# Routing of two expert layers: places with experts on partitions, slots ahead of the gates, router products in two column halves

## The chip, the cores and the metric

The kernel runs on one core of a Trainium2 chip: TensorE (PE; PEld is its weight load), VectorE (DVE), ScalarE (ACT), GpSimd (POOL), SyncE (SP, which here only issues DMAs), and 16 DMA engines. The metric is the device time of one execution in microseconds (us). Lower is better.

## The reference, cut to what matters

Two transformer blocks in a row on 512 tokens of width 1024 in fp32. Each block ends in a routed expert layer:

```python
# block 1: 32 experts in 4 groups; a token takes the best group and its two best experts
gates = jnp.sum(jax.nn.one_hot(e_idx, N_EXPERTS) * e_weight[..., None], axis=1)
...
hid = silu(hf @ w_g[e]) * (hf @ w_u[e]) * gates[:, e]
out = out + hid @ w_d[e]
# block 2: 64 experts in 8 groups, six experts a token, and one expert that all tokens share
shared = (jax.nn.silu(xf @ w_sh_gate) * (xf @ w_sh_up)) @ w_sh_down
return (shared + routed).reshape(B, S, D)
```

Every expert has three matrices of 1 MB (1024 x 256, 1024 x 256, 256 x 1024), so the first layer reads 96 MB of weights and the second 192 MB. Everything in front of the expert layers (attention of two kinds and a gated recurrence in block 1, two attentions and modulation in block 2) is untouched by the change.

## The kernel before

The 512 tokens are four tiles of 128 rows (`NT`). An expert layer is one `Moe` object: `phase_b` builds the one of 32 experts, `phase_d` with `rest_d` that of 64.

Router. As each tile of the residual is done, `head(t)` normalises it and writes it to DRAM (`hD`); the tile is transposed on PE (`xt`) and `logits(t)` multiplies it by the router's weights: eight fp32 matmuls a tile with the 128 x 128 token block as the weights in the array and 36 (block 1) or 64 (block 2) columns moving (bank `lg`). VectorE then picks groups and experts and leaves a one-hot matrix, `A` in block 1 and `Ab` in block 2, tokens on partitions, and the gates `G`.

Places. `positions` counts the tokens of each expert (`cnt`), and `rank` sorts the experts by their counts into a permutation matrix `P`; `perm` (its list) lets SP address the weights of the expert of rank r. Static loads (the first `STATIC` experts) need no `perm`. `positions` then makes each token's place within its expert: ten bf16 matmuls (`pos`), `posm`, four transposes (`posT`), a copy, a matmul by `P` that sorts the rows by rank (`posR`) and a cast. `ranked` transposes the gates (`GT`), sorts them by rank (`Gr`) and writes them to DRAM (`gD`).

Units. The experts are worked in units of 128 slots, `UNITS1` and `UNITS2`; a unit is shared by one to three experts of known ranks (64 + 64, 96 + 32, ...). `pick(u)` makes a matrix `sel` that names the rank of each slot, `prep(u)` calls `slots`: `bc` broadcasts the place row of each slot's expert (one fp32r matmul), VectorE compares it with the slot's number (`st`) and sums the token number out of it (`jk` is the scratch output, `ii` the number), and two indirect DMAs on POOL's queue gather the 128 token rows (`xg` from `hD`) and their gates (`gg` from `gD`). `turn` transposes the rows on PE (`xT`); `hidden` multiplies by the gate and up matrices (`g`, `u`), takes silu on ScalarE and the product with the gate on VectorE (`hid`), and transposes that (`hT`); `down` makes `y`; `scatter` adds it back with `st` as the matrix (`sc`).

Order. The code is written once in an order and a planner, run when the program is built, fixes each engine's queue from it: an instruction that is ready and stands earlier in the code goes first, `high_priority` moves a part up, `issue_after` puts one behind another, and `manual_schedule` keeps the units' PE and VectorE queues as written. Tiles live in rooms by tag: all tiles of a tag share its buffers. Of pool `moe` matter here: `hid` (one buffer; the tiles `hid` and `jk`), `xT` (one buffer; `xT`, and in block 2 the shared expert's `hTx`), `st` (four), `yh`, `yl` and `sel` (two each). `Carve` lends the rooms of `st`, `yh` and `yl` to the router's small tiles until the units need them. PSUM has two rings of four banks, `bank` and `pbank`; `lg`, `g`, `u`, `y` and the shared expert's `hT` come from `pbank`.

In block 1, `rest` calls `positions`, `ranked` and `run`. `run` picks and preps units 0 and 1, then lets `fetch(3, after=self.gathered.ins, free=NF)` release the rest of unit 2's loads: a one-element memset on POOL in each weight buffer stands behind the last gather of unit 1, and the load behind the memset. In block 2, `rest_d` calls `positions` and `ranked`, then traces the shared expert (`hidden` and `down` over four tiles), and only then `run`. The shared expert needs the normalised tiles (`hTs`) and nothing of the routing.

## Time and profile before

| | |
|---|---|
| time, median of 3 runs | 1671.65 us (1668.68 to 1672.71) |
| the profiled execution's own time | 1676.92 us |
| its span, first to last instruction | 1675.2 us |
| granted TensorE clock, mean share of full | 0.971 |
| busy: PE, PEld, DVE, ACT, POOL | 93%, 63%, 58%, 32%, 21% |
| DMA | 420.78 MB, mean 251 GB/s |
| first expert layer: router to the last unit | about 350 to 610 us |
| second expert layer: router to the end | about 1055 to 1675 us |

A share of busy time is a mean over the whole span. The stages differ, so the stages are read by their own windows and timelines. A matmul counts as busy from its start to its modelled end, so a PE that is busy throughout may still be waiting for its clock, which has two levels here, 1.0 (2.4 GHz) and 0.5 (1.2 GHz).

### The profile page before, as it was taken

The page shows a single profiled execution, that of the slowest core. Times are in us where ns is not written, and L with a number is a line of the kernel's source. Part 1 is how long each engine was busy: PE and PEld are TensorE (multiplying, and loading weights), DVE is VectorE, ACT ScalarE, POOL GpSimd, SP SyncE. Part 2 cuts the span into 40 slices and gives each one's busy share as a digit, 9 for nine tenths or more (in the row PEclk, how much of TensorE's full clock was granted, in tenths as well). Part 3 has the DMA queues.
Part 4 walks back from the last instruction along what each step waited for, and adds up shares of the span by engine and source line. Part 5 has one row for each costly group of instructions (what it writes and reads, how often), then busy time and mean ns, then how long its engine had stood idle before and what let it go on. Part 6 is the DMA issues. An engine that isn't in the chain of part 4 may idle for free.

```text
span 1675.2 us, 28638 instructions
## 1 busy us (share of the span) xinstructions
PE 1550.9 (93%) x10917; PEld 1060.7 (63%) x10917; DVE 970.1 (58%) x2219; ACT 542.3 (32%) x1090; POOL 347.4 (21%) x287
## 2 busy tenths in 40 slices
PE   5899999978998877899999998999999999999996
PEld 5665557765565546675667777865666666666663
DVE  3598536853564348547455534555665665656656
ACT  4534676331211125555553322301211211112112
POOL 2323551012111103330104441131111101111000
PEclk9999999987999998999999999899999999999998
DMA  5443336468999953233006837748899999999961
GB/s 187 147 162 114 107 82 233 132 214 321 418 416 417 419 239 105 72 104 90 26 5 203 255 104 276 285 168 366 366 411 386 396 412 415 418 414 422 419 259 64
DMA packets 104207, 420.78 MB, mean 251 GB/s; under 512 B 23444, under 2 KB 30074, under 8 KB 66692
## 3 DMA queue, kind: packets, MB, share of 16 engines
q1 hardware_dynamic: 82880, 389.25, 60.5%
q0 software_dynamic: 9968, 19.04, 3.1%
q10 hardware_dynamic: 11220, 10.63, 2.0%
q8 instruction: 87, 1.43, 0.3%
q14 instruction: 52, 0.43, 0.1%
HBM read 419.99 MB, written 9.21 MB: 256 GB/s over the span
## 4 chain that ended last, share of the span: by engine, by line
PE 46%; DVE 5%; DMA 4%; POOL 1%; ACT 1%; issue 1%; SPq 0%; DVEq 0%; ACTq 0%; POOLq 0%
PE g L973 8%; PE u L973 8%; PE sc L1051 7%; PE y L997 7%; PE qk L1671 2%; DMA mw<-in_w_mod_dram 2%; PE ob L1699 2%; PE xT L938 2%; PE pt L110 1%; PE pt L109 1%; PE pt L108 1%; PE pt L1691 1%; DVE macc L1400 1%; POOL wl L137 1%; DMA gmr<-in_g_ffn_norm_dram 1%
## 5 line engine op out<-in xcount | busy, mean ns | idle before, releaser
L137 POOL TENSOR_TENSOR wl<-w,wh 128x1024 fp32r<-128x1024 f32 (+4 forms) x72 | 166.7, 2316 | 366.4 <-ACT wh L136 343.9
L1052 DVE TENSOR_TENSOR xres<-xres,sc 128x512 f32<-128x512 f32 x368 | 224.5, 683 | 4.2 <-PE sc L1051 1.0
L973 PE MATMUL u<-wu,xT 128*32 128x256 f32 (+2 forms) x2240 | 180.4, 388 | 12.3 <-DMA wu<-in_w_exp_up_dram 10.0
L973 PE MATMUL g<-wg,xT 128*32 128x256 f32 (+2 forms) x2240 | 177.9, 383 | 1.1 <-DMA wg<-in_w_exp_gate_dram 1.1
L915 POOL DMA_INDIRECT xg<-hD,ii x46 | 46.1, 1001 | 609.4 <-issue 504.3
L997 PE MATMUL y<-wd,hT 128*32 128x512 f32 (+2 forms) x1120 | 167.6, 596 | 0.0
L973 PEld LDWEIGHTS u<-wu,xT 128*32 128x32 f32 (+2 forms) x2240 | 120.8, 121 | 61.5 <-DMA wu<-in_w_exp_up_dram 12.4
L979 DVE SCALAR_TENSOR_TENSOR hid<-u,gc,hid 128x256 f32<-128x256 f32 x46 | 22.3, 484 | 236.4 <-PE u L973 236.4
L973 PEld LDWEIGHTS g<-wg,xT 128*32 128x32 f32 (+2 forms) x2240 | 103.8, 119 | 86.4 <-issue 33.7
L1051 PE MATMUL sc<-yh,st 128*128 128x512 f32 x368 | 152.2, 416 | 0.0
L136 ACT ACTIVATE wh<-w 128x1024 fp32r<-128x1024 f32 (+4 forms) x88 | 89.9, 1021 | 184.2 <-PE pt L109 81.6
L1051 PE MATMUL sc<-yl,st 128*128 128x512 f32 x368 | 144.4, 395 | 0.1
L987 ACT ACTIVATE hT<-hT 128x256 f32<-128x256 f32 x46 | 17.7, 384 | 299.7 <-PE hT L984 299.7
L116 ACT ACTIVATE yh<-y 128x512 fp32r<-128x512 f32 x92 | 54.9, 597 | 162.8 <-DVE y L1005 104.7
L108 PE MATMUL pr<-wh,xh 128*128 128x512 f32 (+2 forms) x256 | 102.1, 403 | 5.7 <-ACT wh L136 5.2
L109 PE MATMUL pr<-wl,xh 128*128 128x512 f32 (+2 forms) x256 | 101.4, 398 | 6.1 <-POOL wl L137 6.1
L997 PEld LDWEIGHTS y<-wd,hT 128*32 128x32 f32 (+2 forms) x1120 | 46.6, 118 | 90.7 <-issue 88.5
L117 DVE TENSOR_TENSOR yl<-y,yh 128x512 fp32r<-128x512 f32 x92 | 63.6, 691 | 67.1 <-ACT yh L116 55.5
L110 PE MATMUL pr<-wh,xl 128*128 128x512 f32 (+2 forms) x256 | 100.6, 397 | 0.2 <-DVE xl L117 0.2
L110 PE MATMUL pt<-xh,wl 128*128 128x512 f32 x224 | 89.4, 399 | 3.0 <-POOL wl L137 3.0
L108 PE MATMUL pt<-xh,wh 128*128 128x512 f32 x224 | 90.3, 403 | 0.3 <-DVE qM L1620 0.2
L109 PE MATMUL pt<-xl,wh 128*128 128x512 f32 x224 | 89.0, 398 | 0.0
(535 smaller groups left out, 2819.2 us busy)
## 6 DMA issues: line engine op xcount, KB each, us to landing
wg<-in_w_exp_gate_dram SPq DMA_DIRECT2D x96, 1024.0 KB
wu<-in_w_exp_up_dram SPq DMA_DIRECT2D x96, 1024.0 KB
wd<-in_w_exp_down_dram SPq DMA_DIRECT2D x96, 1024.0 KB
w<-in_w_in_dram SPq DMA_DIRECT2D x52, 512.0 KB
mw<-in_w_mod_dram SPq DMA_DIRECT2D x32, 512.0 KB
mw<-in_w_mod_dram SPq DMA_DIRECT2D x8, 1024.0 KB
w<-in_w_out_dram SPq DMA_DIRECT2D x16, 512.0 KB
brs<-brd ACTq DMA_DIRECT2D x1, 2560.0 KB
```

Of the source, the lines that this page charges most:

```text
L108: nc.tensor.matmul(out, lhsT=lh, rhs=rh, start=first, stop=False)
L109: nc.tensor.matmul(out, lhsT=lh, rhs=rl, start=False, stop=False)
L110: nc.tensor.matmul(out, lhsT=ll, rhs=rh, start=False, stop=last)
L116: hi = nc.scalar.activation(dh, src, AF.Copy)
L117: lo = nc.vector.tensor_sub(dl, src, dh.bitcast(F32))
L136: nc.scalar.activation(wh[:, :, :c], w[:, :, :c], AF.Copy)
L137: (eng or nc.gpsimd).tensor_sub(wl[:, :, :c], w[:, :, :c], wh[:, :, :c].bitcast(F32))
L915: self.gathered = nc.gpsimd.indirect_dma_start(out=x, out_offset=None, in_=src, in_offset=bass.IndirectOffsetOnAxis(ap=ii[:, :1], axis=0), ...
L973: nc.tensor.matmul(b[sl], lhsT=xT[:, kk, sl], rhs=g[h][:, kk], start=kk == 0, stop=kk == KD - 1)
L997: nc.tensor.matmul(b[sl], lhsT=hT[:, j, sl], rhs=d[:, j, h * 512:(h + 1) * 512], start=j == 0, stop=j == 1)
L1051: nc.tensor.matmul(b, lhsT=st[:, ts], rhs=y[h][i], start=i == 0, stop=i == 1)
L1052: nc.vector.tensor_add(self.acc[:, t, hs], self.acc[:, t, hs], b)
```

## The change

The tokens' places are made with the experts on the partitions from the start: the one-hot block is now the weights, a triangular matrix `places` (`upper` with 512 on the diagonal, in place of the sum and product of `posm`) moves, and ScalarE copies the result to `posT`; this stands ahead of `rank`. The sorting by rank is done by `pick`, which copies columns of `P` in place of columns of the identity. A new `begin` picks and preps units 0 and 1 between `positions` and `ranked`, with the row gathers in place and the gate gathers kept back in a list `late`, which `run` works off first. `begin` also holds block 1's `fetch(3, ...)`. In block 2 it stands ahead of the shared expert. `Carve` in block 2 fills `yh` and `yl` first, and four tiles that `ranked` needs are made early. `GT` is copied by ScalarE.

The router's products trade their operands: 64 columns of router weights (block 1's are padded with zeros from 36) are the weights, and the token block's 128 columns move; even and odd blocks of the contraction go to the two column halves of the array. ScalarE copies the two halves (`part`), and one matmul with `sum2` (two identities) adds and transposes them. A second bank of `pbank` is taken for that. Constants that count from one now count from 512 (`PICKED`), in the spill path too; `posT`'s memset goes, and a memset of the padding comes.

```diff
-        P = self.P = m.tile([E, E], F32, name="P")
+        P = self.P = self.x.tile([E, E], F32, name="P")
...
-        nc.vector.tensor_copy(GT, b[:E])
+        nc.scalar.activation(GT, b[:E], AF.Copy)
...
+        b = k.bank("pos")
+        for t in range(NT):
+            for j in range(t + 1):
+                nc.tensor.matmul(b[:E, t * 128:(t + 1) * 128], lhsT=Ab[:, j], rhs=k.places if j == t else k.ones,
+                                 start=j == 0, stop=j == t)
+        self.posT = self.x.tile([E, S], F32R, name="posT")
+        nc.scalar.activation(self.posT, b[:E], AF.Copy)
         self.rank(m, perm)
...
-        b = k.bank("pos")
-        for t in range(NT):
-            for j in range(t + 1):
-                nc.tensor.matmul(b[:, t * E:(t + 1) * E], lhsT=k.upper if j == t else k.ones, rhs=Ab[:, j],
-                                 start=j == 0, stop=j == t)
-        posm = m.tile([128, NT, E], F32, name="posm")
-        nc.vector.scalar_tensor_tensor(posm, b[:, :NT * E].rearrange("p (t e) -> p t e", t=NT), 1.0, Ab,
-                                       op0=ALU.add, op1=ALU.mult)
-        self.posT = self.x.tile([128, S], F32R, name="posT")
-        nc.gpsimd.memset(self.posT.bitcast(F32), 0.0)
-        b = k.bank("posT")
-        for t in range(NT):
-            nc.tensor.transpose(b[:E, t * 128:(t + 1) * 128], posm[:, t], k.ident)
-        pe = m.tile([E, S], F32, name="posE")
-        nc.vector.tensor_copy(pe, b[:E])
-        b = k.bank("posR")
-        nc.tensor.matmul(b[:E], lhsT=self.P, rhs=pe, start=True, stop=True)
-        nc.vector.tensor_copy(self.posT[:E], b[:E])
...
+    def slots(self, sel, iota, base, xg, late=None):
...
-        for x, src in zip(xg, (self.hD, self.gD)):
-            self.gathered = nc.gpsimd.indirect_dma_start(out=x, out_offset=None, in_=src,
+        def get(i):
+            self.gathered = nc.gpsimd.indirect_dma_start(out=xg[i], out_offset=None, in_=(self.hD, self.gD)[i],
                                                          in_offset=bass.IndirectOffsetOnAxis(ap=ii[:, :1], axis=0),
                                                          bounds_check=S - 1, oob_is_err=False)
+        get(0)
+        if late is None:
+            get(1)
+        else:
+            late.append(lambda: get(1))
...
     def pick(self, u):
 
-        sel = self.sel[u] = self.m.tile([128, 128], F32R, tag="sel", name="sel", bufs=2)
+        E = self.E
+        sel = self.sel[u] = self.m.tile([128, 128], F32R, tag="sel", name="sel", bufs=2)[:E]
         o = 0
         for w, r, _ in self.units[u]:
-            self.k.nc.vector.tensor_copy(sel[:, o:o + w], self.k.ident[:, r:r + 1].to_broadcast([128, w]))
+            self.k.nc.vector.tensor_copy(sel[:, o:o + w], self.P[:, r:r + 1].to_broadcast([E, w]))
             o += w
...
-    def run(self):
-        n = len(self.units)
+    def begin(self):
+
+        late = []
         for u in range(2):
             self.pick(u)
-        self.prep(0)
-        with self.k.tc.issue_after(self.indexed.ins):
-            self.prep(1)
+            self.prep(u, late)
         if self.E == 32:
             self.fetch(3, after=self.gathered.ins, free=NF)
-        self.take(0)
+        return late
+
+    def run(self, late):
+        n = len(self.units)
+        for f in late:
+            f()
+        self.xT[0] = self.turn(self.xg[0][0])
         self.pick(2)
+        self.gates(0)
         self.prep(2)
         self.table()
...
+    k.places = pool.tile([128, 128], BF, name="places")
+    nc.vector.tensor_scalar(k.places, k.causal, -1.0, None, op0=ALU.is_lt)
+    nc.vector.scalar_tensor_tensor(k.places, k.ident, float(PICKED), k.places, op0=ALU.mult, op1=ALU.add)
+    k.sum2 = pool.tile([128, 64], F32, name="sum2")
+    nc.vector.tensor_add(k.sum2, k.ident[:, :64], k.ident[:, 64:])
...
+def router(k, part, acc, out, t, wr, xT):
+
+
+    nc, ts = k.nc, slice(t * 128, (t + 1) * 128)
+    for kk in range(KD):
+        q = 64 * (kk % 2)
+        nc.tensor.matmul(acc[q:q + 64, ts], lhsT=wr[:, kk], rhs=xT[:, kk], start=kk < 2, stop=kk >= KD - 2)
+    nc.scalar.activation(part, acc[:, ts], AF.Copy)
+    nc.tensor.matmul(out[:, t * 64:(t + 1) * 64], lhsT=part, rhs=k.sum2, start=True, stop=True)
...
-        for kk in range(KD):
-            nc.tensor.matmul(lbs[0][:, t * 36:(t + 1) * 36], lhsT=xTs[:, t % 2, kk], rhs=wr[:, kk], start=kk == 0,
-                             stop=kk == KD - 1)
+        router(k, p.tile([128, 128], F32, name="part"), lbs[0], lbs[1], t, wr, xTs[:, t % 2])
...
         moe.positions(A, v, perm)
+        late = moe.begin()
         moe.ranked(G, v, p)
-        moe.run()
+        moe.run(late)
...
-        for kk in range(KD):
-            nc.tensor.matmul(lb[:, t * E:(t + 1) * E], lhsT=hT[:, kk], rhs=wr[:, kk], start=kk == 0, stop=kk == KD - 1)
+        router(k, gmr[:, 1, 512 + 128 * t:640 + 128 * t], lbs[0], lbs[1], t, wr, hT)
...
-    p = Carve(moe)
+    p = Carve(moe, (("yh", 2), ("yl", 2), ("st", 4)))
...
+    for name, shape in (("G2", [128, NT, E]), ("GT", [E, S]), ("n4", [128, NT]), ("ce", [E, 2])):
+        p.made[name] = p.tile(shape, F32, name)
...
     nc.vector.tensor_mul(Gt, Gt, n4[:, :, None].to_broadcast([128, NT, E]))
+    late = moe.begin()
     moe.ranked(Gt, p, f)
...
         moe.down(hTx[:, t], ws, add)
-    moe.run()
+    moe.run(late)
```

## Rows read from the trace of the kernel before

**Rows 1.** Windows of the first layer: start:end, length, busy us of PE, PEld, DVE, ACT, POOL (instructions), clock, DMA share, GB/s

```profile
366.00:400.00 34.00, 19.32 (x107) 11.49 (x109) 15.26 (x72) 3.28 (x6) 9.25 (x18) 0.57 0.53 193
...
400.00:600.00 200.00, 189.53 (x1649) 112.69 (x1648) 98.54 (x217) 36.19 (x71) 25.10 (x22) 0.97 1.01 418
```

**Rows 2.** Timeline of the first layer's routing: start us, us, engine, line, operation, tile, times

```profile
361.60 4.09 PE L1271 MATMUL lg<-misc,xTs 128*128 128x36 f32 x32
...
371.12 0.29 DVE L1322 TENSOR_TENSOR A<-cv 128x128 bf16<-128x128 f32 x1
...
373.73 0.23 DVE L841 TENSOR_SCALAR cv<-tok,cv 32x32 f32<-32x32 f32 x1
...
376.19 1.04 SPq L802 DMA_DIRECT2D wg<-in_w_exp_gate_dram  x2
...
378.77 1.04 PE L855 MATMUL GT<-ident,cv 128*32 128x128 f32 x4
...
382.61 1.22 PE L903 MATMUL bc<-posT,sel 128*128 128x512 f32 x2
...
385.06 0.14 DVE L913 TENSOR_SCALAR ii<-ix 128x1 int32<-128x1 f32 x1
...
385.48 1.13 POOL L915 DMA_INDIRECT xg<-hD,ii  x1 [12.81 <-DVE ii L913]
...
389.03 1.95 PE L938 MATMUL xT<-ident,xg 128*128 128x128 f32 x8 [5.20 <-DMA xg<-hD,ii]
...
390.54 0.15 POOL L789 MEMSET wu<- 128x1 f32 x2
...
391.85 3.67 PE L973 MATMUL g<-wg,xT 128*64 128x256 f32 x14
...
397.68 0.09 POOL L789 MEMSET wd<- 128x1 f32 x1
...
407.18 3.62 PE L973 MATMUL g<-wg,xT 128*64 128x256 f32 x32
```

**Rows 3.** Tile xg from 370 to 470 us: its seven gathers, issue to landing

```profile
DMA to landing us min/median/max: 3.4/9.4/10.0
```

**Rows 4.** Windows of the second layer, columns as in the first group

```profile
1062.00:1068.00 6.00, 6.00 (x28) 5.53 (x27) 6.00 (x8) 2.23 (x4) 2.36 (x1) 0.50 0.43 175
...
1068.00:1072.00 4.00, 4.00 (x20) 3.66 (x20) 0.38 (x5) 0.77 (x2) 0.00 (x0) 0.60 0.68 215
...
1160.00:1200.00 40.00, 40.00 (x390) 26.44 (x387) 22.49 (x49) 7.67 (x15) 5.96 (x6) 1.00 0.94 386
```

**Rows 5.** Timeline of PE in the second layer's routing

```profile
1074.13 3.68 PE L1891 MATMUL lg<-gmr,hT 128*128 128x64 f32 x32
...
1084.59 0.51 PE L984 MATMUL hT<-ident,hid 128*128 128x128 f32 x2 [0.59 <-DVE hid L977]
...
1084.93 3.62 PE L973 MATMUL g<-sg,hT 128*128 128x256 f32 x16
...
1092.83 0.51 PE L984 MATMUL hT<-ident,hid 128*128 128x128 f32 x2 [0.83 <-DVE hid L977]
...
1113.46 13.90 PE L997 MATMUL y<-sd,hTx 128*128 128x512 f32 x32
```

**Rows 6.** Timeline of ScalarE and VectorE in the second layer's routing

```profile
1082.69 0.38 ACT L1911 ACTIVATE cv<-lg 128x256 f32<-128x256 f32 x1 [1.10 <-PE lg L1891]
...
1084.11 0.42 DVE L977 TENSOR_TENSOR hid<-u,hid 128x256 f32<-128x256 f32 x1 [8.21 <-PE u L973]
...
1084.45 0.41 DVE L1913 TENSOR_TENSOR cv<-cv,br 128x256 f32<-128x256 f32 x1
...
1095.54 0.42 DVE L1954 TENSOR_TENSOR Ab<-cv 128x256 bf16<-128x256 f32 x1
...
1112.98 0.74 DVE L906 TENSOR_SCALAR st<-bc,cols 128x512 fp32r<-128x512 f32 x1
...
1115.99 0.68 DVE L911 SCALAR_TENSOR_TENSOR jk<-st,tok 128x512 bf16<-128x512 f32 x1
```

More of the change, by code (lines that the diff above doesn't have):

```diff
@@ L657 @@
 BIG = 4096.0
+PICKED = 512
 NB = 64
@@ L729, in consts_moe @@
     cols[:, 0] = p
-    cols[:, 2] = p + 1
+    cols[:, 2] = PICKED + p
     cols[:, 3] = p % 4 * 128
@@ L738, in consts_moe @@
             for w, _, first in unit:
-                cols[o:o + w, FIRST[E] + u] = first + 1 + np.arange(w)
+                cols[o:o + w, FIRST[E] + u] = PICKED + first + np.arange(w)
                 o += w
@@ L1123, in table @@
             for j in range(c + 1):
-                nc.tensor.matmul(b[:, c:c + 1], lhsT=k.upper if j == c else k.ones, rhs=flb[:, j:j + 1],
+                nc.tensor.matmul(b[:, c:c + 1], lhsT=k.places if j == c else k.ones, rhs=flb[:, j:j + 1],
                                  start=j == 0, stop=j == c)
@@ L1150, in spill @@
             ws = [(128, self.load([ev])[0])]
-            sel = m.tile([128, 128], F32R, name="selx")
-            nc.vector.tensor_scalar(sel, row[:, 2:3].to_broadcast([128, 128]), k.cols[:, 0:1], None, op0=ALU.is_equal)
+            sel = m.tile([128, 128], F32R, tag="sel", name="selx", bufs=2)[:E]
+            nc.vector.tensor_scalar(sel, row[:E, 3:4].to_broadcast([E, 128]), k.cols[:E, 0:1], None, op0=ALU.is_equal)
             xg = self.xg[0]
@@ L1172, in __init__ @@
         self.used = [0] * len(self.rooms)
+        self.made = {}
     def tile(self, shape, dt, name=None):
+        if name in self.made:
+            return self.made[name]
         n = math.prod(shape[1:])
@@ L1201, in moe_consts @@
         setattr(k, n, t)
-    k.upper = pool.tile([128, 128], BF, name="upper")
-    nc.vector.tensor_scalar(k.upper, k.causal, -1.0, None, op0=ALU.is_lt)
-    k.lower = pool.tile([64, 64], F32, name="lower")
+    k.places = pool.tile([128, 128], BF, name="places")
[3 more added lines that the diff above has]
+    nc.vector.tensor_add(k.sum2, k.ident[:, :64], k.ident[:, 64:])
+    k.lower = pool.tile([64, 64], BF, name="lower")
     nc.vector.scalar_tensor_tensor(k.lower, k.causal[:64, :64], -1.0, k.ident[:64, :64], op0=ALU.is_gt, op1=ALU.subtract)
@@ L1279, in head @@
             return
-        if t == 0:
+        if t < 2:
             lbs.append(k.pbank("lg"))
@@ L1869, in head @@
     def head(t):
-        if t == 0:
+        if t < 2:
             lbs.append(k.pbank("lg"))
@@ L1898, in rest @@
         moe.work()
-        rest_d(k, out, moe, lbs[0], br, f, perm, hTs, shared, ctx)
+        rest_d(k, out, moe, lbs[1], br, f, perm, hTs, shared, ctx)
     return gm, head, rest
```

22 lines of the change are left out of this document (11 added, 11 removed).

## The prediction

> **What bounds the kernel now.** I read the page's busy shares first: TensorE (PE) is at 93%, but that is a mean over stages with different limits, so I went on to the busy times by stretch around the two expert layers, the only places the change touches. The reader should see two different limits there. In the first layer (32 experts), from 400 to 600 us the DMA engines are full (share 1.01) while PE has some 10 us of gaps: that stretch is a stream of weights, and it ends earlier only by starting earlier. Ahead of it, from 366 to 400 us, both are half idle: DMA 0.53, clock 0.57 [rows 1]. So the first layer's routing is pure latency. In the second layer (64 experts) PE is busy without a gap (40.00 of 40 us in the stretch shown) [rows 4]: what is lost ahead of it is never given back, and what is won counts only if PE's queue gets shorter. Then I followed both routings through the timeline.
>
> First layer: the one-hot A is written at 371.12, the ranking matrix P at 373.73, then come the places (posT, posR), the transposed gates and their ranking (GT, Gr), the broadcast bc at 382.61, the row numbers ii at 385.06, the gather at 385.48, the transposes of the gathered rows at 389.03, the first expert matmul at 391.85 [rows 2]. All of it is one chain.
>
> Second layer: PE does not wait for that chain. The shared expert needs no routing, and its products g and u of four token tiles fill the time in which VectorE ranks; its down-projections y (13.90 us) follow [rows 5]. The routing there is hidden.
>
> **The change, first layer.** Its own steps:
>
> Router products. Now 32 instructions for two tiles take 4.09 us in the first layer, 3.68 in the second [rows 2, 5], 0.115 to 0.13 apiece although their moving operands are 36 and 64 columns, so the weight load sets the pace. After it they have 64-column weights and 128 moving columns, in two halves of the array. The nearest row has 64-column weights and 256 columns: 32 in 3.62 us, 0.113 apiece [rows 2]. If columns set that pace, half of them cost 0.057, 0.9 us a tile; if the load does, 1.8 us, no gain. Added per tile are a copy on ScalarE (a 256-wide one takes 0.38 [rows 6], this is 128 wide) and two instructions with full weights (0.23). The copy stands between them and, for the last tile, on the path; the halves of all tiles share one bank, which I expect to put each copy ahead of the next tile's products. I take 1.5 us earlier for the first layer, 1.0 for the second, with bounds of 3 us earlier and 1 later each.
>
> The Trainium skill, "TensorEngine Tiling (Array Packing)", When to Use Tiling, recommends this very swap for a right-hand side of at most 64 columns and promises up to two times. No row of this trace has the swapped form; by the rule a tile would save its half, 0.94 us, less the 0.23 added, 2.8 us a layer, and the sum below would be 1678.5 in place of 1681.6.
>
> Places. Posm, four transposes, a copy, posR and a cast go; ten counting matmuls come right behind the counts, 128 columns wide. Bounds for them: nothing, and four 128-column fp32 transposes in the same slow stretch take 1.04 [rows 2], so ten up to 2.6. I take 1.1, as the operands are bf16; that ends about when the ranking's key is ready anyway, and their copy (some 0.7, twice the 256-wide one) is done before pick is. At 2.6 the ranking waits 1.5. Then, counted from A's start at 371.12: P ends 2.84 later (373.96); pick(0)'s two copies, formerly ahead of all this, now wait for P, each at most as long as P's own write (0.23), I take 0.3 for both; bc start to ii end is 2.59 now (382.61 to 385.20), with 0.1 of handover 2.7; the gather issues 0.28 after ii. Sum 6.1 in place of 14.36, so 8.2 earlier; I take 7.9 (6.7 to 8.3) [rows 2].
>
> The gather then falls on other traffic. The ranking releases two loads of 1 MB at 376.19 [rows 2]; at 418 GB/s [rows 1] they take 5 us, and some 3.5 are left when the gather issues. Unloaded it landed 3.4 us after issue, in the full stream it takes 9.4 [rows 3]. Bounds: 0 to 6 us more; I take 1.6, since only part of two loads is ahead. The first expert matmul moves by 7.9 - 1.6 + 1.5 = 7.8 us.
>
> Also moved past others: the gathers of the gates come last on POOL, behind both row gathers and behind the ranked gates' write from ScalarE's queue. The POOL memsets that free the next two up loads, at 390.54 behind the fourth gather, come behind the second: about 10 us earlier, so DMA has no hole to fill. The later slots free only as unit 0's g ends (memset at 397.68), which moves by the 7.8 [rows 2]. A ceiling: DMA's idle share of this stretch is 0.47 of 34, 16 us, of which up to 10 lie ahead of the ranking's loads [rows 1], so without the router's part no less than 6 and no more than 16 can be won; 6.3 lies inside. The unit-0 gates then arrive close to their use; late, they would cost up to 3 us of this. **First layer: 7.8 us earlier (2 to 10.5).** The deleted memset of posT, GT's copy moved to ScalarE, and the wider memsets and constants lie off this chain (POOL is busy for 9 and ScalarE for 3 of its 34 us [rows 1]).
>
> **The change, second layer.** Here the same move adds a wait. jk, the scratch output of slots, and hid, the shared expert's hidden rows, share one room (tag hid, one buffer). Slots used to be traced behind the shared expert; now jk(0) and jk(1) stand ahead of hid(0). Does the planner hand a room out in the order of the code? The trace says yes for the PSUM ring: g of tile 1 starts only behind hT of tile 0, after PE idled 0.59 us, and the same at 1092.83 after 0.83, though the router had read those token tiles by 1077.8 [rows 5]. A ring handed to whoever is ready would have let g go. So I infer that silu(0) must wait for jk(1), the end of the whole routing chain. Behind it on PE stand hT(0), the other three tiles' g and u, and every y; on ScalarE the copies of hTx; and the first unit waits for the last y. Only g(0) and u(0) fill the time.
>
> How long: the sigmoid starts at 1082.69, 1.0 earlier by the router. The next sum on VectorE waited until 1084.45 behind hid(0) (1084.11); freed of that it starts at 1082.2 (the sigmoid's end at 1083.07, 0.15 of handover, less the 1.0). From its start to Ab's end is 11.5, less one further hid product of 0.4: 1093.3. Then counts, places and P 2.8 as above; pick, bc (two take 1.22) and handovers 1.7; and from st to the second jk's end 3.7 (1112.98 to 1116.67): jk(1) ends at 1101.5 [rows 6]. Silu, product and handovers 1.0: PE resumes with hT(0) at 1102.5, where it did at 1084.59.
>
> What is left there: from hT(0) to hT(1) are 8.24 us, 7.4 without the wait, for one hT, one g (3.62) and one u; three such, the last hT (0.5) and y (13.9) make 36.6 [rows 5]. Of the former 42.8 (1084.59 to 1127.36) the rest, 0.8 of that wait and 5.4 of the routing's matmuls, now lies in the gap or is gone. hT's waits, no longer filled: three at 0.7, 2.1. And PE comes back slow. In the first layer a mean clock of 0.57 over 366 to 400 puts its rise from 0.5 at 395.2, six us behind the restart at 389.03 [rows 1, 2]; in the second it stood at 0.50 until 1068 and at 0.60 on the mean to 1072 with PE busy throughout, so it rose at 1071.2, over nine us in [rows 4]. Six to ten us at half speed cost 3 to 5; I take 4. y ends at 1102.5 + 36.6 + 2.1 + 4 = 1145.2, not 1127.4. **Second layer: 17.8 us later (10 to 21).**
>
> **Sum.** -7.8 + 17.8 = 10.0 us later. The profiled execution took 1676.92 us (1.7 of it around the span of 1675.2, unchanged), so 1686.9 there; the median of the runs is 5.3 lower, so 1681.6.
>
> **Rivals.** (1) The room is not held back, or silu goes ahead of jk: faster. PE stays filled, loses posT, posR and part of the router's work (2 to 4 us), and with the first layer's 7.8 the kernel takes about 1661. For it: every dependence but that room allows it. Against: the order of g and hT, twice in the rows [rows 5]. It decides from the point where g(1) runs under the ranking. (2) The first layer's gain is lost: the row gathers take the loaded 9.4 us, and the unit's product waits for its gates; 2 us are left of 7.8, and the kernel takes 1687.4. For it: two loads ahead of the gather, two more behind it; against: DMA empties between them. (3) The hold is shorter: two free banks let g(1) and u(1) go ahead (7 us) and the clock stays up (4 us); 6.8 us lost, 7.8 won, no change, 1670.7. Against: the same two rows.
>
> **How the numbers follow.** Forecast 0.57 (own range 1676 to 1688), rival 1 0.15, rival 2 0.15, rival 3 0.13. A measurement tells about 0.3%, 5 us, from nothing. Slower than 1676.7: nearly all of the forecast, rival 2 and a little of rival 3, 0.73; within: the rest of both, 0.12; faster: rival 1, 0.15. The range leaves out rival 1 and the forecast's far tail: 1668 to 1689.
>
> **What would show it.** In the changed trace: the first layer's row gather about 9 us closer behind A than now, and DMA full from about 382 us. In the second layer no g of the shared expert between about 1084 and 1100 us, a silu directly behind the second jk, hT(0) at 1100 to 1104, and the granted clock at 0.5 in that hole. If g and u run on under the ranking there, the step on the room is wrong and the kernel is faster. If the row gather lands 9 us behind its issue, rival 2 holds.

## The result, and the profile after

The changed kernel takes 1693.8 us (median of 4 runs, 1689.47 to 1694.72), the kernel before 1671.64 in the same series (1668.68 to 1672.71): a ratio of 1.0115, 95% interval 1.0091 to 1.0139, so 15 to 23 us slower. Forecast were 1681.6 us and at most 1689: the sign is right, the size is not. One step holds (the second layer loses 18 us, forecast 17.8), one does not (the first layer wins 1 us, forecast 7.8).

**First layer.** The timeline of the changed kernel's routing, merged from the queues of VectorE, PE and POOL, answers to [rows 2] (start us, us, engine, line, operation, tile, and in brackets the idle time before with its releaser):

```profile
356.69 1.03 PE L1286 MATMUL xt<-ident,xres 128*128 128x128 f32 x8
...
361.56 0.43 PE L1229 MATMUL lg<-sum,part 128*128 128x64 f32 x2 [0.44 <-ACT part L1228]
361.93 1.09 PE L1227 MATMUL lg<-xTs,misc 128*64 128x128 f32 x16
...
369.32 0.33 DVE L1340 TENSOR_TENSOR A<-cv 128x128 bf16<-128x128 f32 x1
...
371.90 0.23 DVE L842 TENSOR_SCALAR P<-tok,cv 32x32 f32<-32x32 f32 x1
...
374.71 0.68 DVE L901 SCALAR_TENSOR_TENSOR jk<-st,tok 128x512 bf16<-128x512 f32 x1
...
377.44 0.29 DVE L861 COPY cv<-Gr 128x128 f32<-128x128 f32 x1 [2.03 <-PE Gr L860]
377.64 0.14 DVE L903 TENSOR_SCALAR ii<-ix 128x1 int32<-128x1 f32 x1
...
378.08 1.31 POOL L905 DMA_INDIRECT xg<-hD,ii  x1 [7.32 <-DVE ii L903]
...
382.98 1.94 PE L934 MATMUL xT<-ident,xg 128*128 128x128 f32 x8 [5.46 <-DMA xg<-hD,ii]
...
385.79 3.67 PE L969 MATMUL g<-wg,xT 128*64 128x256 f32 x14
...
389.49 0.31 DVE L944 COPY gc<-gg 64x1 f32<-64x1 f32 x2 [10.38 <-DMA gg<-gD,ii]
...
391.40 0.14 DVE L903 TENSOR_SCALAR ii<-ix 128x1 int32<-128x1 f32 x1
...
391.73 0.18 PE L1126 MATMUL ov<-flb,places 128*128 128x1 bf16 x1 [2.26 <-DVE flb L1122]
...
392.28 0.99 POOL L905 DMA_INDIRECT xg<-hD,ii  x1 [7.44 <-PE ov L1129]
...
394.88 1.03 POOL L1138 DMA_INDIRECT tbl<-rw,ati  x1 [0.31 <-issue]
395.92 0.11 POOL L790 MEMSET wd<- 128x1 f32 x1
```

Read from A: the gather is issued 8.76 us behind A's start. Before it was 14.36, forecast 6.1. Of the missing 2.7, 2.1 are at 377.44: VectorE's queue has the copy of the *ranked gates* between jk(0) and its ii (a kernel without that, below, has 6.66). The slots are written ahead of the gates in the code, but the planner filled VectorE's wait with the gates' copy, which itself waits 2 us for PE. From the issue to xT are 4.9 us (forecast 5.0), and the first g comes 16.47 behind A, before 20.73.

The gain of 4.3 then runs into the last rows. The gates now arrive last (their copy gc is at 389.49). Behind that copy VectorE has the third unit's slots, whose row numbers ii come at 391.40, and the overflow table's flags (flb), for which PE's `ov` waits in the middle of g (2.26 us of idle). POOL then works off, one behind the other, the third unit's two gathers (from 392.28; they read that ii, though the bracket names another), the table's scatter and the memset that lets the next wd load go. That memset is 26.60 us behind A; in [rows 2] it was 26.56. That the two agree so closely is chance, for before the third unit's slots waited not for the gates but for PE's bc, which came behind the first unit's transposes:

```profile
391.44 0.75 DVE L906 TENSOR_SCALAR st<-bc,cols 128x512 fp32r<-128x512 f32 x1 [1.84 <-PE bc L903]
```

Nothing of the gain has reached the queue of weights: the stretch in which the DMA engines are mostly idle (share 0.29 and 0.27) has only moved, from 383 to 391 us before to 391 to 397 us. Those two stretches and windows of 44 us from A, first the kernel before, then the changed one (columns as in [rows 1]):

```profile
383.00:391.00 8.00, 2.80 (x11) 2.00 (x10) 3.65 (x16) 0.60 (x1) 4.32 (x7) 0.50 0.29 69
...
371.12:415.12 44.00, 33.79 (x212) 19.98 (x213) 15.35 (x60) 5.91 (x10) 10.85 (x18) 0.72 0.71 270
```

```profile
391.00:397.00 6.00, 5.27 (x38) 3.26 (x40) 1.25 (x13) 1.67 (x2) 3.13 (x4) 0.69 0.27 83
...
369.32:413.32 44.00, 33.53 (x208) 20.93 (x209) 13.75 (x60) 7.08 (x12) 10.94 (x18) 0.71 0.76 288
...
1080.00:1100.00 20.00, 6.66 (x34) 4.73 (x34) 16.44 (x62) 1.78 (x3) 0.17 (x1) 0.60 0.24 99
```

The last two figures of a row are the DMA share and GB/s: 44 us at 270 are 11.9 MB, weights for the most part, at 288 12.7 MB. From there DMA is full in both, so 0.8 MB are some 2 us at the 418 GB/s of [rows 1].

**Second layer.** Its row in that fence, 1080 to 1100, shows the hole: PE busy for 6.66 of 20 us at a mean clock of 0.60. The changed kernel's timeline there, for [rows 5, 6]:

```profile
1089.92 0.43 DVE L1975 TENSOR_TENSOR Ab<-cv 128x256 bf16<-128x256 f32 x1
1090.40 0.37 PE L875 MATMUL cnt<-ones,Ab 128*64 128x1 bf16 x4 [11.28 <-DVE Ab L1975]
...
1098.54 0.42 DVE L861 COPY cv<-Gr 128x256 f32<-128x256 f32 x1 [2.04 <-PE Gr L860]
1098.94 0.68 DVE L901 SCALAR_TENSOR_TENSOR jk<-st,tok 128x512 bf16<-128x512 f32 x1
...
1099.41 1.28 ACT L971 ACT_TABLE_LOAD   x1 [2.92 <-DVE ii L903]
1100.70 0.38 ACT L971 ACTIVATE hid<-g 128x256 f32<-128x256 f32 x1
...
1101.60 0.70 PE L980 MATMUL hT<-ident,hid 128*128 128x128 f32 x2 [2.79 <-DVE hid L973]
1102.09 4.88 PE L969 MATMUL g<-sg,hT 128*128 128x256 f32 x16
...
1127.93 13.90 PE L993 MATMUL y<-sd,hTx 128*128 128x512 f32 x32
```

As forecast, PE stands still for 11.28 us until VectorE has Ab, silu comes behind the second jk, and the second g of the shared expert starts at 1102.09 and takes 4.88 us instead of 3.62 while the clock is still low (0.50 on the mean from 1084.2 to 1104.6 us). Not in the forecast are the copy of the ranked gates, which stands ahead of the second jk here too and waits 2.04 us for PE, and the load of ScalarE's table (1.28 us) between that jk and silu. y is 14.47 us behind its place in [rows 5], in an execution that was 3.0 us ahead of the first when the last wo product ended.

**Stages over all traces.** Two executions of one kernel differ by several us before the change is reached, so a pair of traces misleads if it is compared by absolute times. The table counts each stage from an event inside the trace: the start of A, the end of the first layer's last scatter product (sc), the end of block 2's last wo product, the start of the first y, the end of the span. MB are those of 44 us from A. The kernels are told below. (Some expectations count to the start of a last product and not to its end, 0.4 us less or more, or to the last y group of the layer, a coarser mark.)

| trace | A at | A to sc | MB | sc to wo | wo to y | y to end | span |
|---|---|---|---|---|---|---|---|
| before | 371.1 | 250.1 | 11.9 | 437.6 | 54.7 | 561.7 | 1675.2 |
| before, second | 375.6 | 248.7 | 12.0 | 439.0 | 53.8 | 556.0 | 1673.1 |
| router only | 369.6 | 250.3 | 12.1 | 441.3 | 51.9 | 555.9 | 1669.0 |
| before, slots ahead | 368.4 | 250.3 | 12.1 | 439.4 | 81.5 | 553.2 | 1692.9 |
| before, table late | 367.9 | 250.1 | 11.8 | 441.6 | 53.8 | 560.6 | 1674.0 |
| changed | 369.3 | 247.8 | 12.7 | 438.7 | 72.1 | 559.4 | 1687.3 |
| changed, second | 370.6 | 249.7 | 12.6 | 442.3 | 72.0 | 559.4 | 1694.0 |
| other room | 366.2 | 251.2 | 12.2 | 442.1 | 59.4 | 562.7 | 1681.5 |
| other room, copy on ScalarE | 367.4 | 247.9 | 12.4 | 441.1 | 57.9 | 562.0 | 1676.3 |
| other room, gates tied | 368.9 | 248.2 | 12.4 | 441.1 | 52.0 | 562.0 | 1672.2 |
| slots behind | 367.2 | 247.9 | 12.5 | 438.2 | 52.5 | 561.7 | 1667.4 |
| slots behind, second | 375.1 | 249.4 | 12.1 | 440.9 | 51.4 | 562.5 | 1679.2 |
| gates first | 369.2 | 249.7 | 11.9 | 441.8 | 51.4 | 562.3 | 1674.4 |
| order kept | 374.1 | 252.5 | 10.9 | 441.5 | 51.4 | 565.1 | 1684.5 |
| table late | 367.5 | 247.2 | 12.8 | 441.2 | 51.4 | 563.8 | 1671.0 |
| order kept, table late | 375.1 | 251.7 | 11.6 | 440.1 | 52.4 | 564.0 | 1683.2 |
| wd free | 370.1 | 246.1 | 14.5 | 442.7 | 51.4 | 561.7 | 1672.0 |
| gates first, wd free | 371.8 | 243.0 | 14.6 | 439.7 | 52.4 | 561.7 | 1668.6 |

### The profile page after: what moved, and what is told of

Read it like the earlier page. It is cut to its first block, busy times and chain, and to the rows that moved or that the text cites. A ratio compares the mean times of both kernels' runs of the same rounds, so it can differ in the third digit from the quotient of the medians.

```text
span 1687.3 us, 28655 instructions
## 1 busy us (share of the span) xinstructions
PE 1546.2 (92%) x10921; PEld 1037.2 (61%) x10921; DVE 967.6 (57%) x2215; ACT 545.3 (32%) x1101; POOL 345.1 (20%) x286
## 4 chain that ended last, share of the span: by engine, by line
PE 47%; DVE 4%; DMA 4%; ACT 1%; POOL 1%; issue 1%; SPq 0%; ACTq 0%; DVEq 0%; POOLq 0%
PE g L969 8%; PE y L993 8%; PE u L969 7%; PE sc L1047 7%; PE qk L1690 2%; DMA mw<-in_w_mod_dram 2%; PE ob L1718 2%; PE xT L934 2%; PE pt L110 1%; PE pt L109 1%; PE pt L108 1%; PE pt L1710 1%; DVE macc L1419 1%; PE bc L893 1%; POOL wl L137 1%; PE hT L980 1%
## 5 line engine op out<-in xcount | busy, mean ns | idle before, releaser
L969 PE MATMUL u<-wu,xT 128*32 128x256 f32 (+2 forms) x2240 | 172.5, 382 | 9.7 <-DMA wu<-in_w_exp_up_dram 7.8
L969 PE MATMUL g<-wg,xT 128*32 128x256 f32 (+2 forms) x2240 | 173.7, 384 | 2.2 <-DMA wg<-in_w_exp_gate_dram 1.6
L969 PEld LDWEIGHTS g<-wg,xT 128*32 128x32 f32 (+2 forms) x2240 | 99.8, 119 | 89.2 <-ACT yh L116 22.2
L969 PEld LDWEIGHTS u<-wu,xT 128*32 128x32 f32 (+2 forms) x2240 | 103.0, 119 | 70.5 <-DMA wu<-in_w_exp_up_dram 10.2
```

The costliest lines, as they stand in the source:

```text
L969: nc.tensor.matmul(b[sl], lhsT=xT[:, kk, sl], rhs=g[h][:, kk], start=kk == 0, stop=kk == KD - 1)
```

## The experiments: the second layer's loss

Each is timed against the kernel before on the same chip in the same series; since that kernel's own median was 1671.6 to 1678.5 us over the series, kernels are compared by their ratios to it, given with the 95% interval.

**Another room for jk.** The first two units' jk goes to the room of hT, idle during the shared expert:

```diff
-        jk = m.tile([128, S], BF, tag="hid", name="jk", bufs=1)
+        jk = m.tile([128, S], BF, tag="hid" if late is None else "hT", name="jk", bufs=1)
```

> The changed kernel with one edit: the products jk of the first two units are written to the room of the units' hT (which the shared expert doesn't use, it has hTx) and no longer to the one that hid uses. Theory (the room is what costs the second layer its time): silu(0) of the shared expert starts beside the routing again, as in [rows 5], near 1081 and not at 1100.7; the first y product comes near 1113 and not at 1127.9; the 15 us that the pair of profiles has left of the loss at the end of the run go away, so 1679 us against the changed kernel's 1693.8, and nearer 1670 if what the two timings differ by beyond the pair of profiles goes with it. Rival (something else holds the shared expert: the ranked gates' copy, a table load, the order of PE's queue): the first y product stays past 1124, and the time within 4 us of 1693.8.

1681.38 us, ratio 1.0050 (1.0031 to 1.0069): 11 us of the 19 are gone (0.65% of 1672). g and u of the shared expert run under the ranking again, y starts 59.4 us behind wo, not 72.1. The room is the cause, but 7.5 us more than the other kernels' 51.4 to 52.5 are left. The timeline shows where:

```profile
1117.37 0.47 DVE L944 COPY gc<-gg 64x1 f32<-64x1 f32 x3 [12.77 <-DMA gg<-gD,ii]
1117.86 0.42 DVE L973 TENSOR_TENSOR hid<-u,hid 128x256 f32<-128x256 f32 x1
...
1118.35 0.70 PE L980 MATMUL hT<-ident,hid 128*128 128x128 f32 x2 [6.21 <-DVE hid L973]
```

The first unit's gates stand ahead of the shared expert's last hid product on VectorE and wait 12.77 us for their gather; PE waits 6.21 us for the product.

**The same, with these copies tied behind that product.**

```diff
-            nc.vector.tensor_mul(hid, b, hid)
+            self.plain = nc.vector.tensor_mul(hid, b, hid)
...
-        self.gates(0)
+        with ExitStack() as c:
+            if self.plain is not None:
+                c.enter_context(self.k.tc.issue_after(self.plain.ins))
+            self.gates(0)
```

> The kernel with jk in the other room and the slots ahead of the shared expert, and in the second layer the first unit's copies of its gates tied behind the shared expert's last hid product on VectorE. In the trace with the other room alone these copies stand ahead of that product and wait 12.8 us for the gates' gather, and PE waits 6.2 us for the product. Theory one (that copy is what the other room leaves of the loss): from the last wo product to the first y product it is 53 to 56 us in place of 59.8, and the time 3 to 6 us under that of the kernel with the other room, within 3 us of before. Theory two (the rest of the loss is elsewhere): 58 us or more for that stretch, and no change in time.

1675.31 us, ratio 1.0014 (0.9995 to 1.0033), and 52.0 us from wo to y. So the second layer's loss has two parts, both shown by taking them away: the room (12.7 us of that stretch) and, coming to light only when the room is free, the first unit's gates in VectorE's queue (7.3 us).

**The kernel before with this order alone.** `run`'s head (pick and prep of units 0 and 1, and `fetch(3)`) becomes `begin`, called behind `ranked` and so ahead of the shared expert:

```diff
     moe.ranked(Gt, p, f)
+    moe.begin()
```

> The kernel before, with its own places, its own router and its own gates, and one edit: in the second layer the slots and gathers of the first two units are written ahead of the shared expert's loops and not behind them. Theory: this order alone, by the room that jk and hid share, brings the loss: silu(0) waits for the second jk, the first y product comes 14 to 20 us after its 1113.5 of [rows 5], and the time is 1684 to 1692 us, against 1671.6. Rival (the loss needs the new places or the late gates as well): 1669 to 1675 us, with the first y product within 3 us of 1113.5.

1699.49 us, ratio 1.0164 (1.0148 to 1.0181), y 81.5 us behind wo. The order alone brings the loss, more than I expected (14 to 20 us of it; 27 came). Two things that the changed kernel hasn't add to it: the old places and the gates stand ahead of the slots (the second jk ends 50.8 us behind wo, in the changed kernel 43.8), and PE's queue has the first unit's transposes ahead of the shared expert's hT. The waits of PE from 1078 to 1142 (line, awaited, us in total, times, longest):

```profile
PE cnt L874 <- DVE Ab L1957: 10.5, 1, 10.5
PE xT L938 <- DMA xg<-hD,ii: 7.2, 1, 7.2
```

**The second layer's slots behind the shared expert again,** the rest as changed (`begin` called where `run` is):

> The changed kernel with its second layer's slots written behind the shared expert's loops again (the first layer's stay ahead of the gates). Theory of the room: the loss of the second layer goes as with the other room, 1674 to 1680 us, and within 4 us of it; the slots of the second layer come later, but the shared expert's down products stand in front of the first unit anyway. Rival (in the second layer the earlier gathers are worth something that the hold hides): this kernel is slower than the one with the other room by 5 us or more.

> The kernel with only the second layer's slots moved behind, once more, for a second trace: its first trace was of its fastest run (span 1667.4, granted clock 0.979), and five of its seven runs were 10 us longer at 0.969 to 0.972. Theory one: the 10 us lie in stretches at the lower clock in front of the first layer's end and the second layer's start, and the milestones show them there. Theory two: the stream of weights is slower over the whole of a layer; then they lie in the even stretches 400 to 600 and 1145 to 1600.

1678.9 us, ratio 1.0030 (1.0009 to 1.0052), 8.5 per mille under the changed kernel's, so some 14 us. From wo to y 52.5 and 51.4 us in its two traces. The second trace's span is 11.8 us longer, but 7.9 of these lie ahead of A, where no edit is. That is nearer theory one, though earlier than it says: this trace has a stretch at the lower clock there (0.78 on the mean from 220 to 240 us, 1.00 in the first trace).

**The changed kernel and the kernel before once more,** for second traces:

> The changed kernel once more, unedited, for a second trace: the first had a span 12.1 us over that of before, the timed runs some 20. Theory one (the second layer's first stretch is what varies): from the last wo product to the first y product this trace has again 72 to 73 us, as the first, and what lies more lies behind y or ahead of 1055. Theory two (the hold's length itself varies with TensorE's clock): that stretch is 76 us or more where the run is 1693 or more.

> The kernel before, unedited, for a second trace. Theory one (the stretches are the kernel's own and only their starting times scatter): from the start of A to the last sc product of the first layer 249 to 250 us as in the four traces with its order, 11.8 to 12.1 MB by A plus 44 us, and from the last wo product to the first y product 52 to 56 us, whatever the span. Theory two (the first trace of before was odd): one of the stretches is off by 3 us or more.

The stretch that the room holds was 72.0 us, as in the first trace, and the kernel before's 53.8. A to sc was 248.7 in the second trace of before, 0.3 below the expected band. The changed kernel's second span, 1694.0, is 6.7 us over its first: 1.3 ahead of A, 1.9 in the first layer, 3.6 between the layers. The pair of first traces (12.1 us apart) understates the difference of the medians (22.2 us) by its choice of executions: that of before took 1676.92 us, 5.3 over its median, that of the changed kernel 1689.47, 4.3 under its own.

## The experiments: the first layer's missing gain

**The router alone in the kernel before** (its two halves, the sum, the padded weights):

> The kernel before with only the router's products in two column halves, their sum and the padded router weights (the extra selection tile of the overflow loop shares a room, for memory; that loop doesn't run here). Theory: the logits come 1.8 us earlier in the first layer and 1.0 in the second; in the first layer the next bound (weight loads) eats part of it: 1669 to 1671.5 us against 1671.6. Rival one: both gains arrive whole at the end, 1668.5 us or less. Rival two: a cost of the router that the pair of profiles doesn't show, such as the sum's part copies on ScalarE in front of the norm's squares: 1673 us or more.

1670.73 us, ratio 0.9984 (0.9970 to 0.9999), 2.7 us under before. The size is about that of the first theory, its places are wrong. By absolute times the logits came 1.8 us earlier in the first layer, but that execution had started the stage earlier. Counted from the transposes of tile 2, of which the kernel before has these rows,

```profile
358.11 1.03 PE L1266 MATMUL xt<-ident,xres 128*128 128x128 f32 x8
358.99 1.87 PE L1271 MATMUL lg<-misc,xTs 128*128 128x36 f32 x16
```

A starts 13.01 us behind `xt` before, 12.57 in its second trace, 12.62 in the kernel before with the slots ahead (all three with the old products), 12.62 with the router alone and 12.63 in the changed kernel: no gain that stands out from the spread of the old products. The Trainium skill, "TensorEngine Tiling (Array Packing)", When to Use Tiling, promises up to two times for a swap like this one; the products do come down from 1.87 to 1.09 us a tile, so the trace agrees for them. But PE's queue has each tile's sum, and with it the wait for its copy, between its products and the next tile's. From the start of the last but one tile's products to the end of the last sum are 3.86 us in the changed kernel (360.03 to 363.89); the products of the last two tiles took 4.09 us before [rows 2] and 3.66 in its second trace. So the chain gets nothing. In the second layer, where PE has the shared expert's products for such gaps, wo to y falls from 53.8 and 54.7 us in the traces of before to 51.9.

**Gates first in both layers,** the new places and router as changed:

> The changed kernel with its slots behind the gates' ranking in both layers, as the kernel before has them; the new places and the router's halves stay. Theory one (in the first layer the order is worth what the trace shows, the gathers ahead of the gates' transposes): the first gather is issued about 3 us later than in the kernel with only the second layer's slots moved behind, and the time is 1 to 4 us more than that kernel's 1678.9. Theory two (the order of the first layer is lost in the weights' stream, whose loads were issued at 398.3 in both profiles): the last y of the first layer stays within 1.5 us of 607 to 610, the time within 2 us of 1678.9.

1676.06 us, ratio 1.0009 (0.9989 to 1.0029). Theory one had it 1 to 4 us slower than with the first layer's slots in front (1.0030, 1.0009 to 1.0052); it isn't slower. The gather is issued 10.27 us behind A, 1.5 later than with the slots first and not 3, yet xT comes at 14.08 behind A, only 0.4 later than the changed kernel's 13.66 (before 17.91). So it's the new places that bring the rows earlier, the order next to nothing. A to sc is 249.7, as before: the end of the layer doesn't see even the 3.8 us.

**The ranked gates' copy on ScalarE** (with jk in the other room):

```diff
-        nc.vector.tensor_copy(G, b[:, :NT * E].rearrange("p (t e) -> p t e", t=NT))
+        nc.scalar.activation(G, b[:, :NT * E].rearrange("p (t e) -> p t e", t=NT), AF.Copy)
```

> The kernel with jk in the other room, and the ranked gates' copy (2 us of VectorE's idle time between the first jk and the first ii) moved to ScalarE. Theory one: ii follows jk, the first layer's gather is issued 2.2 us earlier (6.5 us behind the start of A, not 8.7), but the weights that unit 3 on waits for are issued by rooms and not by this: the last y of the first layer moves by under 1 us and the time stays at 1680 to 1683 us. Theory two: the whole 2.2 us arrive, in each of the two layers the first unit is earlier, and the time is 1677 to 1679.5.

1684.22 us, ratio 1.0060 (1.0034 to 1.0086), and the gather still 8.76 us behind A: both theories missed. The planner put the next thing that waits for PE, the copy of the ranked counts, into the same place:

```profile
375.66 0.15 DVE L866 COPY cr<-ce 32x2 f32<-32x2 f32 x1 [2.15 <-PE ce L864]
375.74 0.13 DVE L903 TENSOR_SCALAR ii<-ix 128x1 int32<-128x1 f32 x1
```

**Both copies tied behind the second ii** (`issue_after(self.indexed.ins)` around them; the second layer's slots behind the shared expert, as in all the kernels from here on):

> The kernel with only the second layer's slots moved behind the shared expert, and in the first layer the two copies of the ranked gates and counts tied behind the second ii on VectorE, so that nothing of the gates stands between jk and ii. Theory one (VectorE's queue holds the gather, and the gather's delay doesn't reach the end of the layer): the first gather is issued 6.2 to 6.8 us behind the start of A and not 8.76, xT comes 2 us earlier, but from the start of A to the last y of the layer it is still 240 to 244 us, since the corner of wd and the overflow table wait for the gates' gather as before; the time stays within 3 us of 1678.9. Theory two (it reaches the end): 236 to 239 us for that stretch, and 1674 to 1677 us.

1682.82 us, ratio 1.0020 (1.0003 to 1.0036). The gather is issued 6.66 us behind A, as expected, but xT doesn't come 2 us earlier: it comes 13.30 us behind A, against 13.66 and 13.38 in the two traces of the changed kernel and 14.08 with the gates first. An earlier gather takes longer here, 6.6 us from issue to xT, 4.9 and 4.6, and 3.8; the ranking's two loads of 1 MB are issued about 5.1 and 5.7 us behind A in all of them, and a gather that comes closer behind them shares the DMA engines with more of them. That it is these loads that hold it is read from the order alone; no run leaves them out. And the layer gets *longer*, 252.5 us. POOL's queue in this kernel:

```profile
380.80 1.31 POOL L912 DMA_INDIRECT xg<-hD,ii  x1 [5.11 <-DVE ii L910]
...
395.15 1.00 POOL L912 DMA_INDIRECT gg<-gD,ii  x1 [11.54 <-DMA gD<-cv]
```

The earlier gathers release the weight loads earlier (SP's up loads 9.4 us behind A, in the changed kernel 11.5). The gates' write to DRAM, issued 8.5 us behind A in both, now goes in among these loads: POOL's wait for it ends 12.5 us after its issue and not 4.8, and all that waits for the gates waits with it: PE's `ov` 5.9 us inside g, the wd corner until 403.99. Only 10.9 MB have come after 44 us.

**The overflow table behind the first unit's down products,** and the third unit's slots ahead of the first unit's gates:

```diff
-        self.gates(0)
-        self.prep(2)
-        self.table()
+        after = []
+        self.prep(2, after)
+        self.gates(0)
+        for f in after:
+            f()
...
+        if u == 0:
+            self.table()
```

> The kernel with only the second layer's slots moved behind, and the overflow table made behind the first unit's down products in place of ahead of the first unit, in both layers; the third unit's slots are ahead of the first unit's gates. Theory one (the first layer's gain is lost because the table's flags wait for the gates' gather, PE's g waits for the flags, and POOL clears wd's corner only behind the table's scatter): the 2.3 us hole in g goes, POOL's clearing of wd's corner comes 3 to 5 us earlier, the DMA share of 392 to 400 rises, and from A to the last y of the first layer it is 236 to 240 us; 1674 to 1677 us. Theory two (the stream's end is set by something else): 240 to 244 us for that stretch, and 1677 to 1681 us.

> Both edits of the two kernels beside it: gates' copies behind the second ii, and the table behind the first unit's down products. Theory one: gather issued 6.2 to 6.8 us behind A, no hole in g, from A to the last y of the first layer 233 to 238 us, and 1670 to 1675 us, the fastest with the new places. Theory two: 240 us or more, and no faster than 1677 us.

> The kernel before, its places and its order as they were, with only the overflow table made behind the first unit's down products. In its trace the table's small product stands in g without a wait of PE, but POOL clears wd's corner behind the table's scatter too. Theory one (that corner delays the stream): 1 to 4 us faster than before. Theory two (before, the gates come with xg and nothing waits): within 1.5 us of before.

1675.7 us, ratio 0.9991 (0.9974 to 1.0008); with the copies tied as well 1680.16, 1.0003 (0.9987 to 1.0020), not the fastest as expected (A to sc 251.7); the kernel before with the late table 1677.28, 0.9993 (0.9979 to 1.0007). The hole in g is gone, but A to sc moves by 0.7 us only: POOL clears the wd corner 25.2 us behind A, 1.4 earlier and not 3 to 5. Only the scatter is gone from ahead of it; it still stands behind the third unit's gathers, whose ii waits on VectorE behind the gates' copy. In the kernel before, nothing.

**That corner left out,** on top of the late table. The second wd load waits for its room alone:

```diff
-            g[i][2] = self.slot([128, 2, D], F32, "wd", after=after)
+            g[i][2] = self.slot([128, 2, D], F32, "wd", after=after if i == 0 else None)
```

> The kernel with the late overflow table and the second layer's slots moved behind, and the second wd of a load that waits for the gathers without a cleared corner on POOL, so that its load waits for its room alone. Theory one (the stretch from A to the end of the first layer follows the megabytes of weights that have come 44 us behind A: 11.9 before, 12.5 with the second layer's slots moved, 12.8 with the late table, at some 0.42 MB/us): SP issues the second wd near 388 to 390 and not 393.2 (21 to 22 us behind A, not 25.7), 13.2 to 14.3 MB have come by A plus 44 us, and from A to the last sc product of the layer it is 243 to 246 us against 246.8; the time is 1 to 4 us under that of the late table alone. Theory two (the room comes free no earlier than POOL clears it): the same 12.8 MB and 246 to 248 us, and no difference in time.

> The same kernel with the first layer's slots behind the gates' ranking again. Theory one (the gates' write and gathers lose to the weights when the tokens' gathers go first, so the gates' order is worth as much as the slots'): from A to the last sc product within 1.5 us of the kernel beside it, and the time within 2.5 us of it. Theory two (the slots' order is worth something once the table and the corner are out of the way): 2 us or more longer in that stretch.

The windows of 44 us from A, the second with the gates first, and ahead of the first the stretch in which the changed kernel's DMA engines idled:

```profile
391.00:397.00 6.00, 5.30 (x45) 3.49 (x41) 2.23 (x7) 2.69 (x5) 1.99 (x2) 1.00 0.94 354
...
370.13:414.13 44.00, 36.05 (x229) 23.26 (x229) 18.61 (x69) 8.08 (x15) 10.90 (x17) 0.79 0.86 330
```

```profile
371.81:415.81 44.00, 35.31 (x229) 22.94 (x229) 18.43 (x69) 8.07 (x15) 10.79 (x17) 0.80 0.85 331
```

330 GB/s, 14.5 MB: SP has issued the second wd 21.4 us behind A, the hole in the stream is closed (DMA share 0.94 where it was 0.27), and A to sc is 246.1 and 243.0 us, 4 and 7 under the kernel before. In the traces this comes near the forecast's 7.8, by the load's release and not by the slots' order, which with the gates first does better, not worse (neither theory had that). The times are 1671.35 (ratio 0.9996, 0.9980 to 1.0013) and 1671.79 us (0.9994, 0.9976 to 1.0012): 13 us or more under the changed kernel even between the nearest ends of the intervals (1.0013 and 1.0091), but most of that is the second layer's order, which these kernels don't have. They are not shown faster than before, nor than the late table alone (0.9991), which was to be beaten by 1 to 4 us. So that the closed hole shortens the layer rests on one trace of each kernel; that it shortens the run isn't shown.

## Why the prediction was right in one half and wrong in the other

- **Second layer, 17.8 us later: right, with its mechanism.** From wo to y 72.1 and 72.0 against 54.7 and 53.8, so 17.4 to 18.3. The sum hid two things that cancel. The router and the places, without the order, shorten the stretch to 51.4 to 52.5 (I gave the router 1.0 us; in the kernel with the router alone it is 2 to 3), and the order costs 20. The room and silu behind the second jk are as written, and another room takes 12.7 us away. That the sum comes out so close is partly luck, since two of its terms are off and cancel. Counted from the end of wo, hT(0) was to come 43.7 us later; it came at 45.8 and 44.7, because of the table load and, in VectorE's queue, the ranked gates' copy. From there to the end of y I had 42.7 us; it took 40.2 and 41.2, mainly because the low clock cost the second g 1.3 us and 2.2 (5.84 us in the second trace), where I had put 4. What I also didn't see is that the first unit's gates would be next in line behind the room.
- **First layer, router 1.5 us earlier: not so**, nothing that stands out from the spread. I had written that each tile's copy would stand ahead of the next tile's products, but the 1.5 us aren't worked out from that. What the products save, 0.78 us a tile (1.87 to 1.09), goes into PE's wait for the copy (0.44) and the sum (0.43). Whether it is the shared bank that sets this order was not tested.
- **First layer, gather issued 6.1 us behind A: 8.76.** P (it ends 2.81 behind A's start, forecast 2.84), pick, bc and jk are right within 0.5. The error is that I took "ahead of the gates" in the code for ahead of the gates in VectorE's queue. Tied so, it was 6.66. That the gather then took 4.9 us to xT, where the sum has 5.0, is luck: the sum is for a gather at 6.1, and the one issued at 6.66 took 6.6. So the 1.6 us that I gave to other traffic was about half of what it costs at that place (3.1, against 3.55 us from issue to xT before), and with the order tied the rows came no more than 0.4 us earlier.
- **First layer, 7.8 us at its end: about 1** (248.7 on the mean of the changed kernel's two traces, which are 1.9 apart, 249.9 on that of the five with the old places). **This is the step that failed**, in these words of it: "DMA has no hole to fill. The later slots free only as unit 0's g ends (memset at 397.68), which moves by the 7.8." I read the memset's time beside the end of g as its cause. On POOL it stands behind the third unit's gathers and the overflow table's scatter, and these wait on VectorE behind the first unit's gates, whose gather this change makes the last of all. It came 26.60 us behind A, before 26.56, and DMA had its hole there (share 0.27 from 391 to 397 us). With this memset and the table out of the way, 14.5 MB came in place of 12.7 and the layer was 4 to 7 us shorter than before in its trace.
- **Sum.** With the first layer at 1 us in place of 7.8, the same sum gives 17 us later, inside the measured 15 to 23. Rival 2 foresaw the loss of the first layer's gain and its 1687.4 is the nearest of the written cases, but its ground, the row gathers at the loaded 9.4 us, isn't what happened (4.9 us from issue to xT; 6.6 at the earliest place); its second half, a product that waits for its gates, is near it.
- **What stays open.** The span behind y is 559 to 565 us in all kernels with the new places, 553 to 562 in those with the old; the two traces of before lie 5.7 apart, so I can't tell whether the new places cost the second layer's units 2 to 4 us. That might be where the 4 to 7 us won in the last two kernels' first layer went, which the medians don't show.

## What to carry to other kernels

When a chain is shortened, don't stop at the chain's own end: look for the instruction that releases the next *load*, find its place in its engine's queue, and ask what stands ahead of it there. A thing written earlier in the code is earlier only in the queues where nothing that waits is planned into its gaps, so read the order off each queue. And compare stages from an event within each trace: two traces of the same kernel differed here by 7.9 us before the edited stage began.

## What the hardware showed unexpectedly

A small write lost its place to large loads: the gates' write to DRAM (64 KB) took 4.5 to 4.8 us from issue to its waiter when the next weight loads were issued 3 us behind it, and 12.4 and 12.5 us in the two kernels in which they were issued 1 us behind it. In the latter the row gathers stood ahead of it too, but in the trace its packets run from 386.2 to 394.3 us, long after the last row packet (388.3), while in the changed kernel they take 1 us (380.8 to 381.9). And one drop of TensorE's clock, far ahead of the edits, goes with a later start of the edited stages: in four of the eighteen traces, of four different kernels (the second of before among them), the granted clock of 220 to 240 us was 0.77 to 0.79 on the mean, in the other fourteen 1.00; in those four A starts at 374.1 to 375.6 us, in the fourteen at 366.2 to 371.8. Why it drops in some executions, no run here tells.
